# Norm operands made by VectorE, sums taken at other places, first squares in steps: a one-core transformer kernel

## The chip, the core and the metric

The kernel runs on one core of one Trainium2 chip. The metric is device microseconds of one execution. The core's engines work side by side, each through its own queue in order: TensorE (PE in the profile; PEld are its weight loads), VectorE (DVE), ScalarE (ACT), GpSimd (POOL) and SyncE (SP, which only starts transfers here).

## What is computed

The input is 256 tokens of 1024 numbers, in 32-bit floating point. Two blocks follow one another. The first is a norm, one wide projection, banded attention beside a gated recurrence, their merge and a feed-forward layer. The second has four more feed-forward layers, a gating unit and a second attention, each behind a norm of its own.

```python
def rmsnorm(x, g):
    var = jnp.mean(x * x, axis=-1, keepdims=True)
    return x * lax.rsqrt(var + 1e-6) * g

x = first_block(x, ...)                      # ends in a feed-forward layer (f0) and a final norm
for i in range(2):                           # second block
    if i == 1:
        k, v = split(rms_norm(x, kv_norm) @ w_kv)
    x = x + 0.5 * swiglu(rms_norm(x, ffn_norm[i, 0]), ...)       # f1, f3
    h = rms_norm(x, mix_norm[i])
    x = x + (chunked_sgu(h) if i == 0 else stick_breaking_attention(h @ w_q, k, v) @ w_o)
    x = x + 0.5 * swiglu(rms_norm(x, ffn_norm[i, 1]), ...)       # f2, f4
return rms_norm(x, final_norm)
```

Ahead of f1 stand two norms in a row: the first block's final norm and f1's own.

## The kernel before

The activations lie transposed, channels on the 128 partitions and the 256 tokens side by side: `X` is four tiles of 128 x 2 x 256. Weights come from memory as one stream of groups, 128 x 2048 numbers each (1 MB), in the order in which they are used (`PLAN`); a group is two chunks of 128 x 1024. TensorE multiplies in a rounded format, so every operand is held in two parts, a rounded high part and the rest as a low part. For a chunk of weights, ScalarE makes the high part (`h`, line 163) and VectorE subtracts it from the chunk (`l`, line 164); `prep` does both. A product is then three matmuls (`mm3`): high with high, high with low, low with high. A chunk is 24 such matmuls of 256 columns, nearly everywhere.

The order on every engine is the order in which the Python code issues the work. `group` issues the matmuls of two chunks; behind the first chunk it calls the hook `mid`, behind the second the hook `end`, and behind each it gives every waiting generator (`spawn`) two steps (`rounds`) and prepares up to `fills` chunks ahead (`refill`; 4 ahead at the start, 7 later). So a generator is a piece of work that is dealt out between the chunks.

A norm is not applied to its input. The layer behind it multiplies the unnormed input, and a factor R for each token is multiplied onto the result. R is found meanwhile:

1. `squares`: ScalarE squares the four tiles (line 274), VectorE adds them up (lines 276 and 277), and `hl_split` splits the sum into two parts in the tile rr: ScalarE copies the high part (line 337), VectorE subtracts (line 338).
2. `token_sums`: two matmuls with a matrix of minus ones (`nones`) sum over the partitions, into every row. VectorE takes the diagonal of the result (line 290) and reduces it (line 291) to one number for each token on a partition. GpSimd raises it to the power -1/2 (line 307, `rpow`).
3. `diag`: VectorE puts the factors on a diagonal (line 296), and `hl_split` makes two parts of it again.
4. `stats_b`: two more matmuls with `nones` spread the factors over all partitions, and ScalarE copies them to the tile R (line 328). Only then can the layer's results be multiplied (`mulR`, line 334).

`stats_a` is step 2 and asks for step 3 two rounds later; a feed-forward layer has four chunks in K order first (`start_k`), then calls `stats_a` behind the fifth chunk and `stats_b` behind the seventh. Three places matter here. In block 1 `squares` is issued as a whole ahead of the first matmuls. At f1 the two norms give two squares, and `early` takes both sums behind the fifth chunk. At the second attention, `stats_a` is issued behind the four chunks of the key and value projection (`kv`), and `diag` in slot 0 of the loop in `stick` that deals out the attention's work.

Of the kernel before, what the change touches and what calls it, by code (L numbers as in the profile page):

```python
# [9 lines left out]
F32 = mybir.dt.float32  # L10
F32R = mybir.dt.float32r
BF16 = mybir.dt.bfloat16
AF = mybir.ActivationFunctionType
ALU = mybir.AluOpType
# [92 lines left out]
class Builder:  # L107
# [163 lines left out]
    def squares(self, src, dst, n=0):  # L271
        nc = self.nc
        for p in range(4):
            nc.scalar.activation(dst[p], src[p], AF.Square)
        for p in range(1, 4):
            nc.vector.tensor_tensor(dst[0], dst[0], dst[p], op=ALU.add)  # L276
        nc.vector.tensor_tensor(dst[0][:, 0, :], dst[0][:, 0, :], dst[0][:, 1, :], op=ALU.add)
        self.hl_split(dst[0][:, 0, :], self.RR[0][:, n, :], self.RR[0][:, n + 1, :])

# [13 lines left out]
    def diag(self, col, s, n=0):  # L293

        d = s[1][:, 1, :]
        self.nc.vector.tensor_tensor(d.rearrange("p (a b) -> p a b", b=128), self.ident.unsqueeze(1).to_broadcast([128, 2, 128]),
                                     col.unsqueeze(2).to_broadcast([128, 2, 128]), op=ALU.mult)
        self.hl_split(d, self.RR[0][:, n + 2, :], self.RR[0][:, n + 3, :])

# [14 lines left out]
    def stats_a(self, pool=None, kv=False, wait=2):  # L314

        nc = self.nc
        self.st = (pool or self.acc)()
        self.R, self.rcol = (self.Rkv, self.rckv) if kv else (self.Rt, self.rc)
        self.token_sums(self.v2, self.st, self.sq)
        nc.vector.tensor_scalar(self.v2, self.v2, -1.0 / D, 1e-6, op0=ALU.mult, op1=ALU.add)  # L320
        self.rpow(self.rcol, self.v2)
        if wait is not None:
            self.spawn(self.later(wait, lambda: self.diag(self.rcol, self.sq)))

# [80 lines left out]

    def start_k(self, kinds, outs, fills=((2, 2), (2, 2))):
        for gi in range(2):
            self.group(kinds, lambda c, h, l, s: self.pe_k(h, l, s[2], self.XS, outs), fills=fills[gi])


    def block1(self):
        nc, dram = self.nc, self.dram
        SA, SL, RR = self.SA, self.SL, self.RR
        g = lambda k: ("norm_mix_g", k)
        for p in range(4):
            self.split_h(p, self.X, g, self.XS)
            self.split_l(p, self.X, g, self.XS)
            self.prep(2 if p == 0 else 1)
        self.squares(self.X, self.sq)

# [337 lines left out]
    def ffn(self, n, fin, fin_l, stats=None, nat=False, more=None):  # L758
        nc = self.nc
# [4 lines left out]
        def ev(j, bank):  # L764
# [7 lines left out]
            else:  # L772
# [6 lines left out]
        self.start_k((("K", f"{n}_in"),) * 2, [b[0][:, 0, :], b[0][:, 1, :], b[1][:, 0, :], b[1][:, 1, :]],  # L779
                     ((2, 2), (0, 0)) if more else ((2, 2), (2, 2)))  # L780
        sa, sbb = stats or (self.stats_a, self.stats_b)
# [69 lines left out]
    def block2(self):  # L851
# [23 lines left out]
        def early():  # L875
            self.st = self.acc()
            self.R, self.rcol = self.Rt, self.rc
            self.token_sums(self.v2, self.st, self.sq)
            nc.vector.tensor_scalar(self.v2, self.v2, -1.0 / D, 1e-6, op0=ALU.mult, op1=ALU.add)
            self.rpow(r1c, self.v2)  # L880
            self.token_sums(s2[:, 2:4], self.acc(), sq2, 4)
            nc.vector.tensor_tensor(s2[:, 2:4], s2[:, 2:4], r1c, op=ALU.mult)
            nc.vector.tensor_tensor(s2[:, 2:4], s2[:, 2:4], r1c, op=ALU.mult)
            nc.vector.tensor_scalar(s2[:, 2:4], s2[:, 2:4], -1.0 / D, 1e-6, op0=ALU.mult, op1=ALU.add)
            self.rpow(s2[:, 0:2], s2[:, 2:4])
            nc.vector.tensor_tensor(self.rc, s2[:, 0:2], r1c, op=ALU.mult)
            self.spawn(self.later(2, lambda: self.diag(self.rc, self.sq), lambda: self.diag(r1c, sq2, 4)))

# [16 lines left out]
        fin, fin_l = self.boundary(0.5, lambda k: ("mix_norm", k))  # L905
        self.ffn("f1", fin, fin_l, stats=(early, sbb), more=True)
        self.squares(self.X, self.sq)
# [28 lines left out]
        def kv_emit(c, h, l, s):  # L936
            kp = s[2]
            XH, XL = KX
            for kk in range(2):
# [5 lines left out]
                for t in range(2):  # L945
# [3 lines left out]
                    self.mm(vb[:, t, :], XL[:, k, ts], h[:, sl], False, k == 7)  # L949

        for gi in range(2):
            self.group((("K", "kv"),) * 2, kv_emit)

        def kv_ev(R=self.R, rcol=self.rcol):
            nc.vector.tensor_tensor(Kt, kb, R.unsqueeze(1).to_broadcast([128, 2, 256]), op=ALU.mult)
            for t in range(2):
                nc.scalar.activation(Vt[:, t, :], vb[:, t, :], AF.Copy, scale=rcol[:, t:t + 1])
            yield
# [157 lines left out]
    def stick(self, Kt, Vt, fin, fin_l):  # L1116
# [65 lines left out]

        self.stats_a(self.wk, wait=None)
        at = lambda f, T: f(T) if 0 <= T < 8 else None
# [47 lines left out]
        for slot in range(17):  # L1232
            at(values, slot - 5)
            next(work, None)
            if slot == 0:
                zero = SL["b"][:, 1536:1664]
                nc.gpsimd.memset(zero, 0.0)
                for i in range(2):
                    for t in (sh[i], sl[i]):
                        nc.vector.tensor_copy(t[:, :, 0:128], zero.unsqueeze(1).to_broadcast([128, 2, 128]))  # L1240
                self.diag(self.rcol, self.sq)
            if slot == 1:
                self.stats_b()
                nc.scalar.preload_act_table_set("natural_log_exp_and_others")
# [130 lines left out]
```

## Time and profile before

| | |
|---|---|
| median of 3 runs (their span) | 1414.47 us (1407.7 to 1415.67) |
| the profiled execution | 1416.44 us, its span 1414.7 us |
| TensorE busy | 1398.4 us, 99% of the span |
| VectorE, ScalarE, GpSimd busy | 969.2, 740.2, 25.6 us |
| chain that ended last | TensorE 94%, VectorE 3%, ScalarE 1% |
| mean transfer rate | 184 GB/s |

The profile is of one execution, and its times count from the start of the span. Busy time of TensorE is modelled from pipelined matmuls, so it can be near 100% and still hide differences in the spacing of matmuls. A wait is named by what ended it. The granted clock is given as a share of full speed (1.00 is 2.4 GHz, 0.50 is 1.2 GHz).

### The profile page before, as it was taken

How to read it: one execution, taken by the hardware profiler on the slowest of the kernel's cores; microseconds unless marked ns; L12 is line 12 of the kernel's file. 1: busy time of each engine (PE TensorE's matmuls, PEld its weight loads, DVE VectorE, ACT ScalarE, POOL GpSimd, SP SyncE). 2: the span in 40 equal slices, each digit the busy share in tenths (PEclk: the TensorE clock that was granted, in tenths of full speed). 3: DMA queues.
4: the chain of work that ended last, by engine and by line, in shares of the span. 5: the costliest groups of instructions: out<-in, count | busy, mean ns of one | idle time of the engine just before them, and what ended most of it. 6: DMA issues, size and time to landing. Idle time of an engine off the chain costs nothing.

```text
span 1414.7 us, 26947 instructions
## 1 busy us (share of the span) xinstructions
PE 1398.4 (99%) x11515; PEld 1356.9 (96%) x11515; DVE 969.2 (69%) x1361; ACT 740.2 (52%) x1112; POOL 25.6 (2%) x57
## 2 busy tenths in 40 slices
PE   8999999999999999999999999999999999999998
PEld 8998999999999999998999999999999998999997
DVE  6977687766667765668685766668656677666663
ACT  5686565554445544446444544446544467544442
POOL 1000000000000000000000000000000000000000
PEclk9999999999999999999999999999999999999999
DMA  8566554655553555556545565554555552445551
GB/s 295 185 201 206 174 195 137 222 185 203 183 205 127 201 199 189 179 194 223 177 151 179 179 224 194 181 204 166 201 217 196 180 179 90 143 171 202 186 188 51
DMA packets 37624, 260.31 MB, mean 184 GB/s; under 512 B 4224, under 2 KB 4608, under 8 KB 7040
## 3 DMA queue, kind: packets, MB, share of 16 engines
q1 hardware_dynamic: 36288, 253.77, 50.7%
q0 software_dynamic: 1072, 4.72, 1.0%
q8 instruction: 90, 1.47, 0.4%
q14 instruction: 30, 0.25, 0.1%
q10 hardware_dynamic: 144, 0.10, 0.0%
HBM read 257.53 MB, written 1.05 MB: 183 GB/s over the span
## 4 chain that ended last, share of the span: by engine, by line
PE 94%; DVE 3%; ACT 1%; issue 1%; DMA 1%; SPq 0%; POOL 0%; POOLq 0%; ACTq 0%; DVEq 0%
PE wk L211 60%; PE acc L211 34%; DVE l L164 1%; DMA raw<-w 1%; ACT h L163 1%; DVE sb L276 0%; DVE xl L267 0%; PE acc L550 0%; DVE x L342 0%; DVE sc L862 0%; DVE sd L276 0%; PE wk L550 0%; DVE x L344 0%; SPq L381 0%; ACT rr L337 0%
## 5 line engine op out<-in xcount | busy, mean ns | idle before, releaser
L164 DVE TENSOR_TENSOR l<-raw,h 128x1024 fp32r<-128x1024 f32 (+1 forms) x479 | 571.5, 1220 | 245.5 <-ACT h L163 245.2
L211 PE MATMUL wk<-xh,h 128*128 128x256 f32 x2272 | 634.1, 279 | 1.7 <-ACT h L163 1.7
L211 PE MATMUL wk<-xh,l 128*128 128x256 f32 x2272 | 631.6, 278 | 1.5 <-DVE l L164 1.5
L211 PE MATMUL wk<-xl,h 128*128 128x256 f32 x2272 | 631.4, 278 | 0.0
L163 ACT ACTIVATE h<-raw 128x1024 fp32r<-128x1024 f32 (+1 forms) x479 | 485.3, 1045 | 39.6 <-PE acc L211 25.8
L211 PEld LDWEIGHTS wk<-xh,h 128*128 128x128 f32 x2272 | 428.1, 188 | 4.8 <-ACT h L163 2.1
L211 PEld LDWEIGHTS wk<-xh,l 128*128 128x128 f32 x2272 | 428.3, 189 | 2.2 <-DVE l L164 2.2
L211 PEld LDWEIGHTS wk<-xl,h 128*128 128x128 f32 x2272 | 429.4, 189 | 0.6
L211 PE MATMUL acc<-rr,h 128*128 128x256 f32 x2016 | 351.2, 278 | 0.0
L211 PEld LDWEIGHTS acc<-rr,h 128*128 128x128 f32 x2016 | 305.1, 188 | 2.1 <-issue 1.9
L211 PE MATMUL acc<-rr,l 128*128 128x256 f32 x1008 | 279.7, 277 | 0.0
L211 PEld LDWEIGHTS acc<-rr,l 128*128 128x128 f32 x1008 | 189.3, 188 | 0.0
L768 ACT ACTIVATE sa<-sa 128x256 f32<-128x256 f32 x110 | 45.4, 418 | 251.2 <-DVE sa L334 250.7
L337 ACT ACTIVATE rr<-sa 128x256 fp32r<-128x256 f32 (+1 forms) x122 | 52.7, 438 | 185.7 <-DVE sa L773 129.1
L334 DVE TENSOR_TENSOR sa<-wk,rt 128x512 f32<-128x512 f32 x92 | 62.3, 686 | 47.7 <-PE wk L211 47.1
L338 DVE TENSOR_TENSOR rr<-sa,rr 128x256 fp32r<-128x256 f32 (+1 forms) x122 | 54.2, 451 | 53.4 <-ACT rr L337 53.4
L211 PE MATMUL acc<-h,rr 128*128 128x512 f32 (+1 forms) x208 | 63.1, 374 | 0.0
L211 PEld LDWEIGHTS acc<-h,rr 128*128 128x128 f32 x208 | 38.5, 188 | 6.6
L262 ACT ACTIVATE xh<-x,par 128x256 fp32r<-128x256 f32 x56 | 25.0, 501 | 31.4 <-DVE x L344 16.2
L211 PE MATMUL acc<-l,rr 128*128 128x512 f32 (+1 forms) x104 | 38.9, 374 | 0.0
L773 DVE TENSOR_TENSOR sa<-sa 128x256 f32<-128x256 f32 x88 | 37.1, 429 | 0.0
L211 PE MATMUL wk<-rr,h 128*128 128x256 f32 x192 | 33.0, 277 | 0.0
(253 smaller groups left out, 995.6 us busy)
## 6 DMA issues: line engine op xcount, KB each, us to landing
raw<-w SPq DMA_DIRECT2D x237, 1024.0 KB, 5.0
sd<-bias POOLq DMA_DIRECT2D x8, 384.0 KB, 3.3
raw<-w SPq DMA_DIRECT2D x3, 512.0 KB, 8.8
sh<-gates SPq DMA_DIRECT2D x1, 1024.0 KB, 8.3
out<-sf SPq DMA_DIRECT2D x4, 256.0 KB, 2.2
x<-x SPq DMA_DIRECT2D x3, 256.0 KB, 8.0
raw<-w SPq DMA_DIRECT2D x2, 256.0 KB, 4.4
sa<-ws POOLq DMA_DIRECT2D x1, 512.0 KB, 3.7
```

The lines of the kernel that those rows point to most:

```text
L163: nc.scalar.activation(h[:, s], raw[:, s], AF.Copy)
L164: nc.vector.tensor_tensor(l[:, s], raw[:, s], h[:, s].bitcast(F32), op=ALU.subtract)
L211: self.nc.tensor.matmul(out, lhsT, rhs, start=start, stop=stop, skip_group_check=True)
L262: self.nc.scalar.activation(xs[0][:, k, :], src[p][:, f, :], AF.Copy, scale=self.par(*g(k)))
L334: self.nc.vector.tensor_tensor(dst, bank, self.Rpair(), op=ALU.mult)
L337: self.nc.scalar.activation(zh, src, AF.Copy)
L338: self.nc.vector.tensor_tensor(zl, src, zh.bitcast(F32), op=ALU.subtract)
L768: nc.scalar.activation(t[:, 0, :], t[:, 0, :], AF.Silu)
L773: nc.vector.tensor_tensor(t[:, 1, :], t[:, 0, :], t[:, 1, :], op=ALU.mult)
```

## The change

Four things change. `two_parts` takes the place of `hl_split` in `squares` and `diag`: VectorE now casts the high part itself. In block 1 `squares_in_steps` is a generator that issues two squares a step, then one add a step, then the split. At f1, `early` keeps the first norm's sums, which move behind the fourth chunk (the new hook `end` of `start_k`); the second norm's sums stay behind the fifth chunk (`sa`), and both diagonals follow at once, the first norm's ahead of the factors' product. At the attention, `stats_a` moves behind the third of kv's four chunks and asks for `diag` two rounds later; `stats_b` stays in slot 1, and the clears of the padding move from slot 0 to slot 1.

```diff
@@ squares @@
-        self.hl_split(dst[0][:, 0, :], self.RR[0][:, n, :], self.RR[0][:, n + 1, :])
+        self.two_parts(dst[0][:, 0, :], n)
+
+    def two_parts(self, src, n):
+        h, l = self.RR[0][:, n, :], self.RR[0][:, n + 1, :]
+        self.nc.vector.tensor_copy(h, src)
+        self.nc.vector.tensor_tensor(l, src, h.bitcast(F32), op=ALU.subtract)
+
+    def squares_in_steps(self, src, dst, n=0):
+        nc = self.nc
+        for p in range(4):
+            nc.scalar.activation(dst[p], src[p], AF.Square)
+            if p % 2:
+                yield
+        for p in range(1, 4):
+            nc.vector.tensor_tensor(dst[0], dst[0], dst[p], op=ALU.add)
+            yield
+        nc.vector.tensor_tensor(dst[0][:, 0, :], dst[0][:, 0, :], dst[0][:, 1, :], op=ALU.add)
+        yield
+        self.two_parts(dst[0][:, 0, :], n)
@@ diag @@
-        self.hl_split(d, self.RR[0][:, n + 2, :], self.RR[0][:, n + 3, :])
+        self.two_parts(d, n + 2)
@@ block1 @@
-        self.squares(self.X, self.sq)
+        self.spawn(self.squares_in_steps(self.X, self.sq))
@@ ffn, start_k: the hook end is called behind the fourth chunk @@
-                     ((2, 2), (0, 0)) if more else ((2, 2), (2, 2)))
+                     ((2, 2), (0, 0)) if more else ((2, 2), (2, 2)), more)
@@ block2 @@
             self.rpow(r1c, self.v2)
+
+        def sa():
             self.token_sums(s2[:, 2:4], self.acc(), sq2, 4)
...
             self.rpow(s2[:, 0:2], s2[:, 2:4])
+            self.diag(r1c, sq2, 4)
             nc.vector.tensor_tensor(self.rc, s2[:, 0:2], r1c, op=ALU.mult)
-            self.spawn(self.later(2, lambda: self.diag(self.rc, self.sq), lambda: self.diag(r1c, sq2, 4)))
+            self.diag(self.rc, self.sq)
...
-        self.ffn("f1", fin, fin_l, stats=(early, sbb), more=True)
+        self.ffn("f1", fin, fin_l, stats=(sa, sbb), more=early)
...
+        R, rcol = self.R, self.rcol
         for gi in range(2):
-            self.group((("K", "kv"),) * 2, kv_emit)
+            self.group((("K", "kv"),) * 2, kv_emit, mid=(lambda: self.stats_a(self.wk)) if gi else None)
@@ stick @@
-        self.stats_a(self.wk, wait=None)
...
-            if slot == 0:
+            if slot == 1:
+                self.stats_b()
                 zero = SL["b"][:, 1536:1664]
...
-                self.diag(self.rcol, self.sq)
-            if slot == 1:
-                self.stats_b()
```

VectorE's order at the start of block 1, before (sb holds the squares, rr_79 the two parts of the sum; l is the low part of a weight chunk):

```order
L164 TENSOR_TENSOR l<-raw,h 128x1024
L276 TENSOR_TENSOR sb<-sb 128x512 x3
L277 TENSOR_TENSOR sb<-sb 128x256
L338 TENSOR_TENSOR rr_79<-sb,rr_79 128x256
L164 TENSOR_TENSOR l<-raw,h 128x1024 x4
L290 TENSOR_TENSOR sb<-acc,ident 128x256
```

And the same place now; the last row takes what the sums' matmuls made:

```order
L164 TENSOR_TENSOR l<-raw,h 128x1024 x2
L294 TENSOR_TENSOR sb<-sb 128x512 x2
L164 TENSOR_TENSOR l<-raw,h 128x1024
L294 TENSOR_TENSOR sb<-sb 128x512
L296 TENSOR_TENSOR sb<-sb 128x256
L164 TENSOR_TENSOR l<-raw,h 128x1024
L283 CAST rr_79<-sb 128x256
L284 TENSOR_TENSOR rr_79<-sb,rr_79 128x256
L164 TENSOR_TENSOR l<-raw,h 128x1024
L310 TENSOR_TENSOR sb<-acc,ident 128x256
```

Three of the l parts that stood behind the two parts of the sum now stand ahead of them, between the adds.

VectorE's order at f1's start, before (sb and sd hold the two norms' squares, v_97 and s_5221 their sums, r1c and rc the factors):

```order
L164 TENSOR_TENSOR l<-raw,h 128x1024 x2
L290 TENSOR_TENSOR sb<-acc,ident 128x256
L291 TENSOR_REDUCE v_97<-sb 128x2
L879 TENSOR_SCALAR v_97<-v_97 128x2
L290 TENSOR_TENSOR sd<-acc,ident 128x256
L291 TENSOR_REDUCE s_5221<-sd 128x2
L882 TENSOR_TENSOR s_5221<-s_5221,r1c 128x2
L883 TENSOR_TENSOR s_5221<-s_5221,r1c 128x2
L884 TENSOR_SCALAR s_5221<-s_5221 128x2
L886 TENSOR_TENSOR rc<-s_5221,r1c 128x2
L296 TENSOR_TENSOR sb<-ident,rc 128x256
L338 TENSOR_TENSOR rr_79<-sb,rr_79 128x256
```

And now, from the second norm's reduction on (the two l parts and the first norm's rows stand ahead of these as before):

```order
L310 TENSOR_TENSOR sd<-acc,ident 128x256
L311 TENSOR_REDUCE s_5221<-sd 128x2
L904 TENSOR_TENSOR s_5221<-s_5221,r1c 128x2
L905 TENSOR_TENSOR s_5221<-s_5221,r1c 128x2
L906 TENSOR_SCALAR s_5221<-s_5221 128x2
L316 TENSOR_TENSOR sd<-ident,r1c 128x256
L283 CAST rr_79<-sd 128x256
L284 TENSOR_TENSOR rr_79<-sd,rr_79 128x256
L909 TENSOR_TENSOR rc<-s_5221,r1c 128x2
L316 TENSOR_TENSOR sb<-ident,rc 128x256
L283 CAST rr_79<-sb 128x256
L284 TENSOR_TENSOR rr_79<-sb,rr_79 128x256
```

The diagonal of r1c, which stood behind rc's, moved with its two parts ahead of the product rc.

TensorE's order at the end of kv, as a difference (acc takes keys and values, rr_81 and rr_82 are kv's input, rr_79 the two parts of the squares' sum):

```order
 L211 MATMUL acc<-l,rr_81 128x256
 L211 MATMUL acc<-h,rr_82 128x256
+L211 MATMUL wk<-rr_79,nones 128x256 x2
 L211 MATMUL acc<-rr_81,h 128x256
 L211 MATMUL acc<-rr_82,h 128x256
```

The two matmuls of the sums, which stood behind kv's fourth chunk, now stand behind its third.

## Rows read from the trace of the kernel before

**Rows 1.** The page, part 1, busy time, share and instructions of each engine.

```profile
PE 1398.4 (99%) x11515; PEld 1356.9 (96%) x11515; DVE 969.2 (69%) x1361; ACT 740.2 (52%) x1112; POOL 25.6 (2%) x57
```

**Rows 2.** Waits of TensorE's queue: total us, times, longest us.

```profile
PE acc L211 <- ACT rr L337: 2.6, 3, 1.2
```

**Rows 3.** Timeline of TensorE, 20.6 to 26 us: start, length, instruction.

```profile
21.31 0.39 PE L211 MATMUL wk<-xh,h 128*128 128x256 f32 x1 [0.38 <-ACT h L163]
...
22.57 0.39 PE L211 MATMUL wk<-xh,l 128*128 128x256 f32 x1 [0.76 <-DVE l L164]
...
25.27 0.40 PE L211 MATMUL acc<-rr,nones 128*128 128x256 f32 x2
```

**Rows 4.** Timeline of ScalarE, 13 to 40 us.

```profile
15.84 2.17 ACT L274 ACTIVATE sb<-x 128x512 f32<-128x512 f32 x4
19.89 0.42 ACT L337 ACTIVATE rr<-sb 128x256 fp32r<-128x256 f32 x1 [1.88 <-DVE sb L277]
```

**Rows 5.** Timeline of VectorE, 13 to 40 us.

```profile
17.12 2.28 DVE L276 TENSOR_TENSOR sb<-sb 128x512 f32<-128x512 f32 x3
```

**Rows 6.** DMA issues between 6.7 and 7.0 us, median us to landing.

```profile
raw<-w SPq DMA_DIRECT2D x1, 1024.0 KB, 10.5
```

**Rows 7.** Groups of instructions of VectorE, shapes apart: count, busy us, mean ns.

```profile
L338 DVE TENSOR_TENSOR rr<-sb,rr 128x256 fp32r<-128x256 f32 x16 | 6.8, 426 | 8.9 <-ACT rr L337 8.9
...
L1240 DVE CAST rr<-sb 128x256 fp32r<-128x256 f32 x4 | 0.9, 287 | 1.0 <-POOL sb L1237 1.0
```

**Rows 8.** Timeline of TensorE at f1's start, 453.9 to 466 us.

```profile
454.15 0.39 PE L211 MATMUL acc<-rr,nones 128*128 128x256 f32 x2
455.48 0.84 PE L211 MATMUL acc<-rr,nones 128*128 128x256 f32 x2 [0.94 <-ACT rr L337]
...
465.34 0.41 PE L211 MATMUL wk<-xh,h 128*128 128x256 f32 x1
```

**Rows 9.** Timeline of VectorE at f1's start, 449 to 466 us.

```profile
450.21 0.42 DVE L277 TENSOR_TENSOR sb<-sb 128x256 f32<-128x256 f32 x1
...
458.69 0.42 DVE L290 TENSOR_TENSOR sb<-acc,ident 128x256 f32<-128x256 f32 x1
...
462.01 0.16 DVE L886 TENSOR_TENSOR rc<-s,r1c 128x2 f32<-128x2 f32 x1 [0.80 <-POOL s L307]
```

**Rows 10.** Timeline of TensorE at the attention's start, 1143 to 1160 us.

```profile
1146.58 0.40 PE L211 MATMUL wk<-rr,nones 128*128 128x256 f32 x2
...
1153.20 0.97 PE L211 MATMUL wk<-rr,nones 128*128 128x256 f32 x2 [2.13 <-ACT rr L337]
...
1159.67 0.70 PE L211 MATMUL wk<-sd,sc 64*128 64x256 f32 x4
```

**Rows 11.** Timeline of VectorE at the attention's start, 1124 to 1172 us.

```profile
1142.90 0.43 DVE L277 TENSOR_TENSOR sb<-sb 128x256 f32<-128x256 f32 x1
...
1144.76 4.63 DVE L164 TENSOR_TENSOR l<-raw,h 128x1024 fp32r<-128x1024 f32 x4 [0.52 <-ACT h L163]
1149.31 0.42 DVE L290 TENSOR_TENSOR sb<-wk,ident 128x256 f32<-128x256 f32 x1
```

**Rows 12.** Windows: us, busy us (instructions) of engines, granted clock, DMA.

```profile
461.70:464.20 2.50, 1.05 (x5) 0.45 (x3) 1.35 (x4) 0.59 (x2) 0.28 (x1) 1.00 0.00 0
464.30:467.60 3.30, 3.10 (x13) 2.93 (x14) 2.60 (x4) 1.97 (x5) 0.00 (x0) 0.50 0.00 0
1153.80:1157.10 3.30, 3.30 (x16) 3.30 (x17) 2.08 (x3) 3.16 (x6) 0.00 (x0) 0.50 0.27 42
20.60:24.00 3.40, 2.26 (x17) 1.86 (x17) 2.88 (x4) 3.40 (x4) 0.00 (x0) 1.00 0.93 369
```

**Rows 13.** Chain in order of time: start us, us, what.

```profile
288.39 5.44 PE acc L211 x48
...
475.04 5.65 PE acc L211 x48
...
616.37 5.65 PE wk L211 x48
```

More of the change, by code (lines that the diff above doesn't have):

```diff
@@ L321, in stats_a @@
         self.rpow(self.rcol, self.v2)
-        if wait is not None:
-            self.spawn(self.later(wait, lambda: self.diag(self.rcol, self.sq)))
+        self.spawn(self.later(wait, lambda: self.diag(self.rcol, self.sq)))
     def stats_b(self):
@@ L404, in view, with start_k @@
         return [t[:, i * w:(i + 1) * w].rearrange("p (a b) -> p a b", b=256) for i in range(n)]
-    def start_k(self, kinds, outs, fills=((2, 2), (2, 2))):
+    def start_k(self, kinds, outs, fills=((2, 2), (2, 2)), end=None):
         for gi in range(2):
-            self.group(kinds, lambda c, h, l, s: self.pe_k(h, l, s[2], self.XS, outs), fills=fills[gi])
+            self.group(kinds, lambda c, h, l, s: self.pe_k(h, l, s[2], self.XS, outs), fills=fills[gi],
+                       end=end if gi else None)
     def block1(self):
@@ L949, in kv_emit, with kv_ev @@
                     self.mm(vb[:, t, :], XL[:, k, ts], h[:, sl], False, k == 7)
+        R, rcol = self.R, self.rcol
         for gi in range(2):
-            self.group((("K", "kv"),) * 2, kv_emit)
-        def kv_ev(R=self.R, rcol=self.rcol):
+            self.group((("K", "kv"),) * 2, kv_emit, mid=(lambda: self.stats_a(self.wk)) if gi else None)
+        def kv_ev():
             nc.vector.tensor_tensor(Kt, kb, R.unsqueeze(1).to_broadcast([128, 2, 256]), op=ALU.mult)
```

## The prediction

> **What bounds the kernel now.** I read the page's share of busy time first: TensorE is busy 1398.4 of 1414.7 us [rows 1]. So a change can win only where TensorE stands still or runs slower than it could, and three views show these places. The list of TensorE's waits is short; its longest row is 2.6 us in three waits for ScalarE's copies into rr, the operands of the norms' sums [rows 2], which the rows of TensorE's order of time place at f1's start [rows 8]; one more such wait of 2.13 us stands at the attention's start [rows 10], and at block 1's start it waits 0.38 us for an h and 0.76 us for an l [rows 3]. The second view is the granted clock: right behind f1's waits and behind the attention's it is 0.50 for a whole stretch, while around block 1's it stays at 1.00 [rows 12]. The third is the chain in order of time: 48 matmuls of 256 columns take 5.44 us in f0 and 5.65 us all the way through f1, both at full clock [rows 13]. The slower spacing (117.7 ns for 113.3 ns) is there from the first such row behind f1's waits to the last one at 616 to 622 us, so a wait can cost more after it than in itself.
>
> **The sum's base** is the profiled execution, 1416.44 us = span 1414.7 + 1.74 around it. The two timed runs near it (1414.47, 1415.67) lie 1 to 2 us lower; the third, 1407.7, is 8.7 lower.
>
> **Two parts by VectorE, everywhere.** Before, ScalarE copies the high part; the copy takes 0.42 us [rows 4], but it waits in ScalarE's queue for VectorE's adds, and every h behind it waits too. After, VectorE casts and subtracts: a cast of this shape takes 287 ns, a subtract 426 ns [rows 7]. Nine squares and nine diagonals (16 of the 18 subtracts are in that row) make 18 casts, 5.2 us more on VectorE in the whole run; it is 69% busy [rows 1], and its l parts are the cover: where I use them below they are ready before TensorE asks. Without that cover, each cast would cost its 0.29 us. Outside the three places TensorE waits for no sums, so there I cost the edit at nothing.
>
> **Block 1's start.** Before, the four squares end at 15.84 + 2.17 = 18.0 us, the copy starts only at 19.89, and the next h (for the fifth chunk) at about 20.3 [rows 4]; TensorE waits for it and its l [rows 3] and takes the sums at 25.27. After, that h comes right behind the squares, 18.0 to 19.05 (its transfer took 10.5 us from about 6.9, so it is there at 17.4 [rows 6]). VectorE makes the l by 20.25, before TensorE asks near 21.0: those two waits go. But the sums' operands come later. VectorE's order now has in front of them an l, two adds, an l, two adds, an l. An l takes 4.63 / 4 = 1.16 us [rows 11], an add 2.28 / 3 = 0.76 [rows 5], the halving add 0.42 [rows 9]: from 20.25 the adds end at 21.7, the l at 22.85, the adds at 23.95, the l at 25.1; cast 25.35, subtract 25.8. TensorE ended the chunk before at 21.31 - 0.38 = 20.93 [rows 3]; matmuls overlap a little, so without the wait the fifth chunk starts near 20.8, and its 24 matmuls are through at 20.8 + 24 x 0.1133 = 23.5. It waits 1.85 us for the high part and another 0.35 for the low, and goes on near 26.0, where before it went on two matmuls behind 25.27, at 25.5 [rows 3]. **Term: +0.5 us**; bounds -0.3 (operands 0.8 sooner) to +2.1 (this wait halves the clock as at f1, where 3.30 us were at 0.50 [rows 12] and so about 1.6 lost). Behind the sums stand the next l and the diagonal, which had 2 us of waits for ScalarE and lose them.
>
> **f1's start.** Before, the first norm's sums run at 454.15, the second's wait for the copy until 455.48, the factors' matmuls wait for two more copies, and the layer's matmuls go on at 465.34, at half clock [rows 8]. After, the first pair stands one chunk earlier, at 454.15 - 24 x 0.1133 = 451.43. Its adds end at 450.63 [rows 9], cast 450.95, subtract 451.4: in time. The second block's adds follow without a copy between: 451.35 to 453.6 and 454.1, cast 454.4, subtract 454.85. TensorE asks for them at 454.4 to 454.5 and waits about 0.4, in place of 0.94 and more. Then two l parts (2.3 us) to 457.1, where the first row of the sums' chain starts; before, that was 458.69 [rows 9], so the chain starts 1.6 us sooner. From there to rc it took 462.01 - 458.69 = 3.3 us, so rc could come at 460.4; the other diagonal with its parts now stands ahead of it, fills the time of the power on GpSimd and holds rc to 460.6; then rc's diagonal, cast and subtract end at 461.25, 461.55 and 462.0. TensorE reaches them at 460.6, waits 1.0 and 0.35, and goes on at 462.5 instead of 465.34: 2.85 us. The clock: before, 1.05 busy of 2.50 us came ahead of the fall [rows 12]; now the idle time is about 1.4 us, as at block 1's start before (2.26 busy of 3.40, no fall), so I take no fall: from 465.34 to 467.6 the 2.3 us at half clock become about 1.2, another 1.05. **Term: -3.9 us**; bounds -2.4 (the clock falls) and -4.7 (no wait for the second pair, and a chain 0.4 shorter).
>
> A rule speaks against this place. The power on GpSimd and the first diagonal now run at once, which no row of before has. The Trainium skill (SBUF — State Buffer, section Who interferes with whom) says that VectorE's two-input operations from SBUF and its two-port casts share a port with GpSimd, and that the later one stands still until the earlier is done. By it the cast would wait out the power and the low part come at 462.7 instead of 462.0, the sum 0.7 us higher. No run here shows it.
>
> **The attention's start.** Before, the sums run behind the kv chunks at 1146.58, but VectorE's reduction waits behind four l parts until 1149.31, and the factors come at 1153.2 after 2.13 us of waiting, with the clock at 0.50 behind it [rows 10 to 12]. After, the sums stand one chunk earlier (near 1143.8). Adds end at 1143.3 [rows 11], cast 1143.65, subtract 1144.1: a new wait of 0.3 us there. Two l parts now stand ahead of the reduction instead of four, and the four clears of the padding go behind the diagonal: reduction 1146.4 to 1147.4, power to 1148.2, an l, diagonal and parts done at 1149.7. TensorE asks at 1151.2: no wait. From 1146.6, where kv ended before, to the first scores (1159.67 before [rows 10]) stand the new wait of 0.3 us, the two matmuls of the sums, two of the factors and 72 of q: 0.3 + 76 x 0.1133 = 8.9 us, so the scores start at 1155.5. **Term: -4.1 us**; bounds -3.0 (half of the wait comes back at the clears or the kv evictions, now behind two l parts) and -4.4 (no new wait).
>
> **Sum:** +0.5 - 3.9 - 4.1 = -7.5, or 1408.9 against the profiled 1416.44; for a timed run of the same kind, about a microsecond lower, **1408**.
>
> **Rivals.** (A) The forecast: the waits shrink, but f1's start still has some, and f1 runs at the slower spacing behind them as before. (B) The same sum, but f1 at the faster spacing: from 463 to 633 us, 170 x (1 - 5.44/5.65) = 6.3 us more [rows 13], **1402**. For it: the spacing is a state that a layer keeps and not a property of its work, since f0 has the same matmuls at the faster one; what sets it at a wait no row shows, so a shorter wait may end in either; and the timed run at 1407.7 is about 7 under its fellows, which this would explain. Against it: it was slow behind both waits of f1 in this trace, and three of four executions of before lie at the high level. (C) The change doesn't make the sums sooner where it counts: f1's chain keeps VectorE's two l parts in front, and the clock falls there and at block 1: +2.1 - 2.4 - 4.1 = -4.4, by the same base **1411**. For it: the same l parts do stand there. (D) The other side: one new wait, the 0.3 us for the sums inside kv or a like one at f2's or f3's start, leaves TensorE at the slower spacing through two layers of f1's length that now run at the faster: 340 x (5.65/5.44 - 1) = +13, so 1408 + 13 = **1421**. It decides once VectorE's parts come later than TensorE's sums there. Against it: outside the three places the chain got shorter by a hand-over, and the sums had no waits.
>
> **Chances.** A 0.44, B 0.42, C 0.10, D 0.04. Half a per cent, 7.1 us of 1414.47 (about what a measurement here can tell from no change), is at 1407.4. B is faster; of A (1406 to 1411, by the terms' bounds) about a quarter lies under that. So faster 0.53, within 0.43, slower 0.04. The range runs from 1400 (B with block 1 at the faster spacing as well, 1 us) to 1412.5 (C and its bound); D and the tails, about 0.15, are left out.
>
> **What would show it.** In the changed profile: no wait for h or l at 21 to 22.6 us but one for the sums near 23.5; VectorE's first reduction in f1 1.6 us earlier against the end of f0; TensorE waits of about 1.4 us in f1 and a clock of 1.00 there; no wait for the factors in attention, scores about 4 us sooner; 48 matmuls in f1 at 5.65 (A) or 5.44 us (B). I am wrong if the clock falls at block 1's new wait, if f1's chain is held by GpSimd, or if the spacing changes in a layer where no wait was.

## The result and the profile after

The changed kernel takes 1402.47 us in the median (14 runs, 1400.62 to 1408.83), the kernel before 1409.84 us (14 runs beside them, 1407.7 to 1415.67). The ratio is 0.9944, with a 95% interval of 0.9926 to 0.9962: faster by 0.56%; the medians differ by 7.4 us. The profiled execution took 1405.7 us, its span 1404.0.

Part 1 of the page, as in [rows 1], and the list of what TensorE's queue waited for, as in [rows 2]:

```profile
PE 1390.9 (99%) x11515; PEld 1350.0 (96%) x11515; DVE 972.4 (69%) x1379; ACT 734.3 (52%) x1094; POOL 26.5 (2%) x57
```

```profile
PE acc L211 <- DVE rr L283: 2.4, 2, 1.6
PE wk L211 <- ACT h L163: 1.3, 1, 1.3
PE wk L211 <- DVE sc L413: 1.1, 1, 1.1
PE wk L211 <- DVE l L164: 1.0, 2, 0.8
PE wk L211 <- ACT sh L1188: 0.5, 1, 0.5
```

The waits for ScalarE's copies into rr are gone (2.6 and 2.1 us). Two waits for VectorE's cast (line 283) remain, one in block 1 and one at f1's start. They stand in TensorE's timeline (start, length, instruction, idle time ahead of it), first block 1, then f1, then the attention:

```profile
22.14 0.28 PE L211 MATMUL wk<-xh,l 128*128 128x256 f32 x1
23.97 0.85 PE L211 MATMUL acc<-rr,nones 128*128 128x256 f32 x2 [1.55 <-DVE rr L283]
24.65 0.28 PE L211 MATMUL wk<-xh,h 128*128 128x256 f32 x1
...
449.92 0.42 PE L211 MATMUL acc<-rr,nones 128*128 128x256 f32 x2
453.03 0.76 PE L211 MATMUL acc<-rr,nones 128*128 128x256 f32 x2
460.07 1.07 PE L211 MATMUL acc<-rr,nones 128*128 128x256 f32 x4 [0.84 <-DVE rr L283]
460.98 0.28 PE L211 MATMUL wk<-xh,h 128*128 128x256 f32 x1
...
1132.01 0.76 PE L211 MATMUL wk<-rr,nones 128*128 128x256 f32 x2
1139.50 0.39 PE L211 MATMUL wk<-rr,nones 128*128 128x256 f32 x2
1143.90 0.93 PE L211 MATMUL wk<-sd,sc 64*128 64x256 f32 x8
```

Where two matmuls of 256 columns take 0.42 or 0.39 us, their operands were there; 0.76 us says that the second pair of f1's sums (453.03) and the attention's sums (1132.01) waited some 0.35 us for their low part. VectorE's timeline shows the chain behind these times: in block 1 the adds between the l parts (line 294 adds in steps, 296 halves), and in f1 the reductions (310), the first diagonal with its parts (316, 283, 284), then rc's.

```profile
18.97 1.41 DVE L294 TENSOR_TENSOR sb<-sb 128x512 f32<-128x512 f32 x2
20.30 1.22 DVE L164 TENSOR_TENSOR l<-raw,h 128x1024 fp32r<-128x1024 f32 x1
21.44 0.68 DVE L294 TENSOR_TENSOR sb<-sb 128x512 f32<-128x512 f32 x1
22.15 0.42 DVE L296 TENSOR_TENSOR sb<-sb 128x256 f32<-128x256 f32 x1
22.50 1.22 DVE L164 TENSOR_TENSOR l<-raw,h 128x1024 fp32r<-128x1024 f32 x1
23.63 0.28 DVE L283 CAST rr<-sb 128x256 fp32r<-128x256 f32 x1
...
455.53 0.42 DVE L310 TENSOR_TENSOR sb<-acc,ident 128x256 f32<-128x256 f32 x1
...
457.96 0.42 DVE L316 TENSOR_TENSOR sd<-ident,r1c 128x256 f32<-128x256 f32 x1
458.41 0.29 DVE L283 CAST rr<-sd 128x256 fp32r<-128x256 f32 x1
...
459.73 0.29 DVE L283 CAST rr<-sb 128x256 fp32r<-128x256 f32 x1
```

GpSimd's second power in f1, which runs beside that first diagonal, and its power in block 1 with the l part that VectorE was at:

```profile
458.13 0.79 POOL L327 TENSOR_TENSOR s<-s,mhalf 128x2 f32<-128x2 f32 x1 [0.76 <-DVE s L906]
...
26.42 1.22 DVE L164 TENSOR_TENSOR l<-raw,h 128x1024 fp32r<-128x1024 f32 x1
...
26.59 1.62 POOL L327 TENSOR_TENSOR rc<-v,mhalf 128x2 f32<-128x2 f32 x1 [23.52 <-DVE v L340]
```

The granted clock (third number from the right) stays at 1.00 behind all three places, where [rows 12] had 0.50 behind f1's and the attention's waits:

```profile
22.20:24.60 2.40, 0.77 (x4) 0.38 (x4) 2.37 (x5) 1.74 (x2) 0.00 (x0) 1.00 1.01 355
...
461.00:464.30 3.30, 3.30 (x32) 3.30 (x31) 3.30 (x7) 2.30 (x7) 0.00 (x0) 1.00 0.45 127
...
1144.00:1147.30 3.30, 3.30 (x30) 3.12 (x31) 1.81 (x2) 2.52 (x5) 0.00 (x0) 1.00 0.57 169
```

The chain in order of time gives the spacing, as in [rows 13]: 48 matmuls take 5.45 us in block 1 behind its sums, 5.44 us all through f1, and 5.65 us in f4, the last layer.

```profile
24.82 5.45 PE wk L211 x48
...
469.31 5.44 PE acc L211 x48
...
605.30 5.44 PE wk L211 x48
...
1222.62 5.65 PE wk L211 x48
1380.63 5.66 PE wk L211 x48
```

**A ledger of all kernels.** TensorE has 11,515 matmul records in every trace. The table takes the starts of the 113th, 346th, 3874th, 5258th, 9644th and last of them, and gives the us between (in the kernel before these starts are at 18.05, 47.06, 470.05, 633.05, 1160.21 and 1407.65 us). No pair of sums crosses such a border. The experiments follow below.

| kernel | block 1 | to f1's start | f1 | to the attention's scores | rest, with f4 | profiled run |
|---|---|---|---|---|---|---|
| before | 29.01 | 422.99 | 163.00 | 527.15 | 247.44 | 1416.44 |
| changed | 28.59 | 419.09 | 156.85 | 523.09 | 252.47 | 1405.7 |
| changed, second | 30.27 | 419.11 | 156.85 | 523.11 | 247.46 | 1402.83 |
| changed, third | 28.60 | 419.10 | 156.85 | 523.07 | 247.44 | 1401.09 |
| parts by VectorE alone | 27.09 | 421.39 | 156.85 | 524.53 | 247.44 | 1403.69 |
| attention as before | 30.18 | 419.25 | 163.00 | 524.63 | 247.44 | 1410.38 |
| f1's start as before | 28.28 | 419.77 | 156.85 | 523.11 | 247.45 | 1401.65 |
| copies by ScalarE | 31.63 | 422.57 | 163.00 | 523.64 | 247.49 | 1414.75 |
| first squares whole | 27.21 | 419.24 | 163.00 | 523.10 | 252.47 | 1411.25 |
| parts behind the l | 26.70 | 419.10 | 156.85 | 523.09 | 247.45 | 1399.72 |
| the same, second | 26.64 | 419.11 | 156.85 | 523.07 | 247.45 | 1399.44 |
| f1's preparations behind | 26.98 | 417.84 | 156.85 | 523.09 | 247.45 | 1399.96 |
| both | 26.68 | 417.85 | 156.85 | 523.07 | 247.44 | 1398.38 |
| both, second | 26.41 | 417.99 | 163.00 | 523.47 | 247.38 | 1404.38 |

Between before and the changed kernel's first profile: 1.23 us ahead of block 1's column (its start lies between 16.82 and 18.95 us in the fourteen profiles; why was not followed), 0.42 in block 1, 3.90 at f1's start, 6.15 in f1, 4.06 at the attention, and 5.03 given back in f4. There is one profile of the kernel before, so how often its clock falls behind f1's and the attention's waits is not shown.

### The profile page after: what moved, and what is told of

It is laid out like the page before. It is cut to its first block, busy times and chain, and to the rows that moved or that the text cites. A ratio compares the mean times of both kernels' runs of the same rounds, so it can differ in the third digit from the quotient of the medians.

```text
span 1404.0 us, 26948 instructions
## 1 busy us (share of the span) xinstructions
PE 1390.9 (99%) x11515; PEld 1350.0 (96%) x11515; DVE 972.4 (69%) x1379; ACT 734.3 (52%) x1094; POOL 26.5 (2%) x57
## 4 chain that ended last, share of the span: by engine, by line
PE 95%; DVE 3%; ACT 1%; issue 1%; DMA 1%; SPq 0%; POOLq 0%; POOL 0%; DVEq 0%; ACTq 0%
PE wk L211 60%; PE acc L211 35%; DVE l L164 1%; DMA raw<-w 1%; ACT h L163 0%; DVE sb L276 0%; PE acc L570 0%; DVE x L361 0%; DVE rr L284 0%; DVE sc L882 0%; ACT sb L290 0%; DVE sd L276 0%; PE wk L570 0%; SPq L400 0%; DVE sb L294 0%
```

## The experiments

All ratios are to the kernel before, from runs on the same chip. The kernels are named as in the table.

**1. Parts by VectorE alone.** Every sum stands where it stood; the first squares are whole.

```diff
 diag, and squares likewise:
-        self.hl_split(d, self.RR[0][:, n + 2, :], self.RR[0][:, n + 3, :])
+        self.two_parts(d, n + 2)
```

> The kernel before with one part of the change: VectorE casts and subtracts both parts of every norm operand; the sums in the second feed-forward layer and in attention stand where they stood, and the first squares are handed out whole. Theory (the gain comes from TensorE's two stalls being taken away by the earlier sums): only the hand-over to ScalarE's copy goes, so TensorE still waits for the second pair of sums and the factors in f1 (together 1.5 to 2.5 us instead of 3.5) and 1.7 to 2.1 us for the factors in attention, with the clock at 0.50 behind the latter; the time is 1 to 2.5 us under before. Rival (the gain comes from ScalarE being relieved everywhere): most of the 7 us is here, 5 to 7 us under before.

Measured: median 1408.25 us (12 runs, lowest 1402.38), ratio 0.9971 (0.9954 to 0.9989). The timeline of TensorE, f1's factors and then the attention's, and the clock in the windows behind them:

```profile
459.06 0.85 PE L211 MATMUL acc<-rr,nones 128*128 128x256 f32 x2 [0.63 <-DVE rr L283]
460.28 0.75 PE L211 MATMUL acc<-rr,nones 128*128 128x256 f32 x2 [0.37 <-DVE rr L283]
...
1141.99 0.84 PE L211 MATMUL wk<-rr,nones 128*128 128x256 f32 x2 [1.21 <-DVE rr L283]
```

```profile
461.30:464.60 3.30, 3.30 (x18) 3.30 (x17) 3.23 (x7) 2.03 (x7) 0.00 (x0) 0.50 0.50 149
1142.00:1145.30 3.30, 3.22 (x26) 3.03 (x27) 2.83 (x4) 2.40 (x4) 0.00 (x0) 1.00 0.26 45
```

The theory's waits are there for f1 (1.0 us in all, where 1.5 to 2.5 was said), but the attention's wait is 1.21 instead of 2.13 us and the clock does not fall behind it. By the table block 1 wins 1.92 us, f1's start 1.60 and the attention 2.62: 6.1 us, more than the theory's 1 to 2.5. Some 1.5 us of the attention's share is the clock that stays up: behind the old wait 16 matmuls took 3.30 us [rows 12], 1.8 us at 113.3 ns each. The timed runs decide less: the ratio is worth 1.6 to 6.5 us, the medians differ by 1.2. In the profiles the rival's size holds; its reason (relief everywhere) does not, since the last column is as long as before, and f1's differs by the spacing alone.

**2. Attention as before** and **3. f1's start as before**, each in the changed kernel.

```diff
 2:
-            self.group(..., kv_emit, mid=(lambda: self.stats_a(self.wk)) if gi else None)
+            self.group(..., kv_emit)
...
+        self.stats_a(self.wk, wait=None)
 3:
-            self.diag(r1c, sq2, 4)
...
-            self.diag(self.rc, self.sq)
+            self.spawn(self.later(2, lambda: self.diag(self.rc, self.sq), lambda: self.diag(r1c, sq2, 4)))
...
-        self.ffn("f1", fin, fin_l, stats=(sa, sbb), more=early)
+        self.ffn("f1", fin, fin_l, stats=(early, sbb), more=True)
```

> The changed kernel, but attention's sums, its diagonal and its clears stand where they stood before. Theory: the factors' wait at the scores is back with 1.7 to 2.1 us and the clock falls to 0.50 behind it, so the stretch from kv's end to the first scores is 3 to 4 us longer than in the changed kernel, and the time 3 to 4 us above it (3 to 4.5 us under before). Rival (ScalarE relieved everywhere): within 1 us of the changed kernel. Second rival (the spacing of the matmuls carries the gain and is set by the stalls): more than 6 us above it.

> The changed kernel, but the sums and diagonals of the second feed-forward layer stand where they stood before. Theory: the waits for the second pair and for the factors are back (about 2 us more idle, and 1 us more if the clock falls to 0.50), and the time is 2.5 to 4 us above the changed kernel at the same spacing of the matmuls. Rival (relief of ScalarE): within 1 us. Second rival (the stall at f1's start sets the slower spacing for the whole layer): 48 matmuls in f1 take 5.65 us again in every execution and the time is 9 to 10 us above the changed kernel.

Measured: attention as before 1408.58 us (12 runs, lowest 1402.38; ratio 0.9977, 0.9954 to 1.0000); f1's start as before 1404.37 us (12 runs, lowest 1401.2; ratio 0.9965, 0.9947 to 0.9983). The stretches are longer than the changed kernel's by 1.54 us at the attention and by 0.67 us at f1's start, both under what the theory said. The attention's wait of 1.21 us is back, with no fall of the clock. At f1 the waits are those of experiment 1 (0.63 and 0.37 us), but here the window behind them is at full clock:

```profile
461.30:464.60 3.30, 3.23 (x26) 3.06 (x27) 3.30 (x6) 1.33 (x4) 0.00 (x0) 1.00 0.16 37
```

So the same waits took the clock down in the profile of experiment 1 (421.39 us to f1's start) and not in this one (419.77): a difference of 1.6 us that the waits don't account for. The medians, 6.4 and 2.2 us above the changed kernel's on that chip (1402.21, experiment 9), are mixed of the groups of runs that experiment 9 is about, so they don't measure these stretches. The second rival, that the stall sets f1's spacing, falls: f1 is at 156.85 us in experiment 3, where its sums stand late again, and at 163.00 in experiment 2, which has f1's start as the change has it. Nor is it the fall of the clock: f1 is at 156.85 us behind the fall in experiment 1, and at 163.00 without one in experiment 2.

**4. Copies by ScalarE**, the reverse of experiment 1: sums and steps as in the change.

```diff
 two_parts:
-        self.nc.vector.tensor_copy(h, src)
-        self.nc.vector.tensor_tensor(l, src, h.bitcast(F32), op=ALU.subtract)
+        self.hl_split(src, self.RR[0][:, n, :], self.RR[0][:, n + 1, :])
```

> The changed kernel with the hand-over left in: ScalarE copies the high part of every norm operand as before, while the sums stand sooner and the first squares in steps as in the change. From the runs so far: at f1's start the stretch from the end of the first chunks to the matmuls behind the factors took 17.03 us before, 13.67 with VectorE's parts alone and 12.95 with both; from kv's end to the scores 15.15, 12.61 and 10.79 us. Theory (each sum waits for the later of two things, and the hand-over is the larger share): f1 15 to 16.5 us, attention 11.5 to 13.5 us, the time 2 to 4 us under before. Rival (the sooner sums alone do it, the hand-over only matters where they stand late): within 1 us of the changed kernel. Second rival (ScalarE's queue holds the sooner copies longer than the later ones): f1 or attention no shorter than before.

Measured: 1406.57 us (12 runs, lowest 1402.95), ratio 0.9981 (0.9959 to 1.0003). At f1's start TensorE still waits for ScalarE's copies, of the second sums and of the factors, and the clock is at 0.50 behind them (467.2 to 470.4 us):

```profile
457.70 0.85 PE L211 MATMUL acc<-rr,nones 128*128 128x256 f32 x2 [0.68 <-ACT rr L354]
465.75 1.08 PE L211 MATMUL acc<-rr,nones 128*128 128x256 f32 x4 [1.55 <-ACT rr L354]
```

Against the kernel before, f1's start wins 0.42 us, the attention 3.51, and block 1 loses 2.62, with a wait of 1.19 us for the copy, one of 0.64 for the low part, and the clock at 0.50 from 26.8 to 30.2 us. In the narrower cut that its expectation uses (3777th to 3874th and 9551st to 9644th record, which a pair of sums worth 0.2 us leaves by standing sooner) f1 takes 16.41 us, in the theory's range, and the attention 11.17, under it; the first rival falls, as the third run of the changed kernel on the same chip has 1401.05 us. Together with experiment 1: at f1's start VectorE's parts alone (no hand-over) give 1.6 us (3.2 without the fall of the clock, by experiment 3), the sooner sums alone 0.4, both 3.9; at the attention 2.6, 3.5 and 4.1, so there either of them does most of it, since either keeps the clock up, which is some 1.5 us of each.

**5. First squares whole** and **6. parts behind the l**, both in the changed kernel.

```diff
 5:
-        self.spawn(self.squares_in_steps(self.X, self.sq))
+        self.squares(self.X, self.sq)
 6:
-        self.spawn(self.squares_in_steps(self.X, self.sq))
+        for p in range(4):
+            nc.scalar.activation(self.sq[p], self.X[p], AF.Square)
+        for p in range(1, 4):
+            nc.vector.tensor_tensor(self.sq[0], self.sq[0], self.sq[p], op=ALU.add)
+        nc.vector.tensor_tensor(self.sq[0][:, 0, :], self.sq[0][:, 0, :], self.sq[0][:, 1, :], op=ALU.add)
+        self.spawn(self.later(2, lambda: self.two_parts(self.sq[0][:, 0, :], 0)))
```

> The changed kernel, but block 1's squares and their adds are handed out whole, ahead of the next h and l. Theory: VectorE's adds come ahead of the fifth chunk's l, so TensorE waits 0.5 to 1 us for that l at 21 to 22 us, and no longer 1.5 + 0.46 us for the sums' operands: the layer gets on 1 to 1.5 us sooner than in the changed kernel. Rival (the steps are a gain, because the wait for the l is longer than that for the sums): TensorE waits 2 us or more there, and the time is 0.5 us or more above the changed kernel.

> The changed kernel, but in block 1 the squares and adds are handed out whole and only the cast and the subtract of the sums' operand stand behind the next l. Theory: with the adds ahead of the fifth chunk's l and its two parts behind it, TensorE waits neither for that l (at most 0.2 us, where it waited 0.7 us with everything whole) nor for the sums, so block 1 gets on about 2.2 us sooner than in the changed kernel: its lowest runs near 1398.5. Rival (the weights' transfers bound this stretch, and a wait taken away here comes back as one for the next h or l): no gain over the kernel with whole squares, lowest runs at 1400.

Measured: whole squares 1403.64 us (12 runs, lowest 1400.06; ratio 0.9959, 0.9939 to 0.9980); parts behind the l 1402.46 us (6 runs, lowest 1399.72; ratio 0.9932, 0.9908 to 0.9956). With whole squares TensorE waits for the fifth chunk's l and then for nothing:

```profile
20.88 0.39 PE L211 MATMUL wk<-xh,l 128*128 128x256 f32 x1 [0.53 <-DVE l L164]
23.49 0.39 PE L211 MATMUL acc<-rr,nones 128*128 128x256 f32 x2
```

Block 1 takes 27.21 us there and 26.70 with the parts behind the l, for 28.6 in the changed kernel (30.27 in its second profile): 1.4 and 1.9 us. The steps cost what the theory said, and the last half microsecond is that wait for the l. The time follows less than was expected of it: the lowest runs are 0.5 and 0.8 us under the changed kernel's 1400.56. In part that is what lies ahead of block 1's column (17.24 and 17.60 us in these profiles, 16.82 to 17.26 in the changed kernel's); the rest is open.

**7. f1's preparations behind** the two diagonals, and **8. both** of 6 and 7.

```diff
-                     ((2, 2), (0, 0)) if more else ((2, 2), (2, 2)), more)
+                     ((0, 0), (0, 0)) if more else ((2, 2), (2, 2)), more)
...
-                           ..., fills=(0, 1) if more and i < 4 else (2, 2),
+                           ..., fills=(2 if i == 2 else 0, 1) if more and i < 4 else (2, 2),
```

> The changed kernel, but the two l preparations that stand ahead of the norm's chain in the second feed-forward layer are handed out behind its two diagonals. Theory (the two l parts hold the chain up): the wait for the factors' matmuls in f1 (1.0 us and 0.35 us for the low part) goes, no wait for an l takes its place, and the time is 1.3 us under the changed kernel at the same spacing. Rival (the l parts are needed at once): TensorE waits 1 us or more for an l in f1 in place of the factors, and the time is the same or longer.

> Both of the last two edits in one kernel. Theory: the gains add up, 2.2 + 1.3 = 3.5 us under the changed kernel, lowest runs near 1397 and the ratio to before about 0.992. Rival (each only moves a wait to a later place): within 1 us of the changed kernel.

Measured: f1's preparations behind 1407.51 us (12 runs, lowest 1399.82; ratio 0.9968, 0.9944 to 0.9991); both 1404.72 us (7 runs, lowest 1398.38; ratio 0.9944, 0.9924 to 0.9964). In the profiles the theory holds: the four factors' matmuls of f1 take 0.62 us with no wait (they are the row below), no l is waited for in their place, and f1's start is 1.25 us shorter than in the changed kernel. With both, block 1 and f1's start are 3.2 us shorter together, of 3.5 expected, and the lowest run is 2.2 us under the changed kernel's.

```profile
459.60 0.62 PE L211 MATMUL acc<-rr,nones 128*128 128x256 f32 x4
```

Yet the medians are above the changed kernel's: most timed runs of both kernels lie 6 us or more over their lowest.

**9. The changed kernel twice more**, **both**, and **parts behind the l** once more each, unchanged.

> The changed kernel itself, once more. Theory (the spacing of the matmuls is set anew in each execution, separately for f1 and for f4, whatever the waits): its runs fall again into groups some 5 to 6 us apart, lowest near 1400.9, and the profile need not show f4 at the slower spacing (48 matmuls in 5.65 us) as the first one did. Rival (the change makes f4 slow and f1 fast): f4 is slow and f1 fast again, and all runs of the first profile's kind lie at one level.

> The kernel with both edits (block 1's two parts behind the next l, f1's preparations behind the diagonals) once more, beside the changed kernel on the same chip. Theory: at the same spacing of the matmuls it is 2.2 us under the changed kernel (lowest runs near 1398.4), while its median moves with the share of runs in which f1 or f4 is at the slower spacing (6.2 and 5.0 us). Rival (the moved preparations make the slower spacing in f1 more frequent): most runs lie near 1404.6 again and the median is no lower than the changed kernel's.

> The changed kernel a third time, as the partner of the last run. Theory: lowest runs near 1400.6, groups 5 to 6 us above; whether f1 or f4 is at the slower spacing in its profile is open (of ten profiles so far f1 was slow in three and f4 in two). Rival: the state belongs to the kernel, and f1 is at the faster spacing as in its two profiles before.

> The kernel in which only block 1's two parts are moved behind the next l, once more, to see whether it beats the changed kernel (28 timed runs: median near 1401.4, 20 of them under 1403.5). Theory: block 1's waits are gone in every execution (no fall of the clock there), lowest runs near 1399.7, and with f1's start left as in the change most runs lie under 1402, so its median is 0.5 to 1.5 us under the changed kernel's. Rival (an earlier arrival at f1 changes how often f1 comes out at the slower spacing, as it did when f1's preparations were moved): half of the runs or more lie near 1405, and the median is above the changed kernel's.

Measured: changed, second 1402.21 us (6 runs; ratio 0.9934, 0.9909 to 0.9959); third 1401.05 us (8 runs; 0.9939, 0.9916 to 0.9963); both, second 1404.63 us (11 runs; 0.9950, 0.9931 to 0.9970); parts behind the l, second 1399.55 us (6 runs, 1399.32 to 1400.07; 0.9929, 0.9911 to 0.9948). The chain of the changed kernel's second profile shows f4 at the faster spacing, where the first had the slower:

```profile
1223.89 5.44 PE wk L211 x48
1377.99 5.47 PE wk L211 x48
```

The chain of both, second, shows f1 at the slower one, from right behind the second pair of sums on and with no wait for the factors:

```profile
421.05 5.44 PE wk L211 x48
451.95 5.65 PE wk L211 x48
466.55 5.65 PE acc L211 x48
...
607.88 5.65 PE wk L211 x48
```

So one kernel comes out at either spacing in f4, and one in f1; the changed kernel's own f1 was at the faster one in all three profiles, as the third run's rival had it. By their times, runs with neither layer slow lie under 1403.5 us in these kernels: 20 of the changed kernel's 28 and 9 of the 12 with the parts behind the l, but only 6 of the 30 in which f1's preparations were moved (experiments 7 to 9; beside one another 7 of 8 of the changed kernel and 2 of 11 of both). The spacing is drawn anew in each execution, then, and the counts speak for the rival, that what stands at f1's start changes the odds. They don't show it: of these longer runs only one was profiled, and the attention as before, whose f1 starts as the changed kernel's does, has 4 of 12 under 1405 us, the like border with its 1.5 us more.

**The better version** is probably parts behind the l. Of the runs with neither layer slow its 9 lie at 1399.32 to 1400.35 us, the changed kernel's 20 at 1400.56 to 1403.48, and block 1 is 1.9 us shorter. That its median is lower too (1399.90 us for 1401.43) is not shown to be its doing: the runs come from different chips, and beside one another the two had 1402.46 and 1402.21. At equal spacing both would be the fastest (lowest 1398.38), but it seldom is at equal spacing.

## Why the prediction was right

The time of 1402.47 us lies in the range, and the terms were said to save 7.5 us and the medians differ by 7.4. The forecast itself, 1408, was 5.5 us too high, by its base and not by its terms; B's 1402 meets the time.

**Block 1, +0.5 us.** The waits for h and l at 21 to 22.6 us went, and one for the sums came: 1.55 us and then about 0.45 for the low part (the pair starts 0.68 us ahead of the next matmul, where two that wait for nothing make 0.23), where the prediction had 1.85 and 0.35, from 23.5 on. The column says -0.42, but in the kernel before these matmuls ran at the slower spacing (48 in 5.65 us at 25.67, against 5.45 at 24.82 in the changed one), which is worth about 0.8 us over the 22 us behind the sums, so +0.4 at like spacing. Whether that spacing is chance is open: of the fourteen profiles the two with ScalarE's copies (before and experiment 4) have 5.65 us there and the twelve others 5.44 or 5.45, so the 0.8 us may be a gain of VectorE's parts that no term had. The upper bound, a fall of the clock, is real too: in the second profile the window behind the same wait is at 0.50, and the stretch takes 30.27 us. First the row of before, then that profile's windows:

```profile
25.67 5.65 PE wk L211 x48
...
22.20:25.50 3.30, 1.63 (x12) 1.23 (x12) 3.23 (x6) 2.00 (x2) 0.00 (x0) 1.00 1.00 370
25.70:29.00 3.30, 3.30 (x17) 3.30 (x17) 2.63 (x6) 0.00 (x0) 1.62 (x1) 0.50 0.70 223
```

What the term hid is that it is a sum of a gain and a loss: VectorE's parts alone make block 1 1.9 us shorter (experiment 1; 1.1 at like spacing), and the steps take 1.5 of it back (28.60 against 27.09).

**f1's start, -3.9 us.** Measured 3.90, and by its steps: no wait for the first pair, 0.35 for the second (0.4 said), 0.84 and about 0.45 for the factors (1.0 and 0.35 said; the four start 0.91 us ahead of the next matmul, where unhindered ones make 0.45), a clock of 1.00. In the trace of before the power's result rc was reached 3.3 us behind the chain's first row; after, 3.55 (455.53 to 459.08), as worked out.

**The attention, -4.1 us.** Measured 4.06: some 0.35 us of wait for the sums' low part (0.3 said), no wait for the factors, full clock. This term and f1's each hold a fall of the clock in the one profile of before (some 1.5 and 1.1 us). None of the seven profiles with f1's start as in the change shows a fall there.

**Two parts elsewhere, nothing.** The rest with f4 takes 247.44 us before and in the profiles with f4 at the faster spacing, and VectorE is at 69% as it was. What the prediction did not see, because it priced each place as a whole, is which edit pays: at f1 and in block 1 it is VectorE making both parts, and not the other edits (experiments 1 and 4).

**The base, and A against B.** This is the step that missed. The sum was set against the profiled 1416.44 us and lowered by a microsecond, on the ground that three of four executions of before lay at the high level. Of 100 runs of before, made beside all these kernels, 58 are at 1410.2 us or under and the median is 1409.6: 1409.6 - 7.5 is 1402.1. The table agrees: the three places give 8.4 us, 7.6 without block 1's spacing. So A's wait was right and A's spacing was not: f1 was at the faster one in all three profiles of the changed kernel, as in B. But B's 6.3 us aren't shown to be a gain of the change: f1 was at the slower spacing in five of the fourteen profiles of the table, with and without waits for the factors, and by its timed runs the kernel before comes near 1408 us too. That the time is B's is thus no proof of B's reason.

**C and D.** C did not come: the chain of f1 came 1.6 us sooner against f0's matmuls, and the clock held at f1. D's price appeared (5.03 us in f4, in a layer with no new wait), but in one of three profiles of the same kernel, so it does not come with the change each time. Two of the prediction's three signs of being wrong thus came, each in one profile of the three: this one, and the fall of the clock at block 1's wait (1.7 us, inside that term's bound).

**The rule on the shared port.** The prediction set the Trainium skill (SBUF — State Buffer, Who interferes with whom) against its sum, for 0.7 us. In f1 the cast at 458.41 lies wholly inside GpSimd's power (458.13 to 458.92) and took its 0.29 us; rc's low part ended 4.95 us behind the chain's first row, where the row sum had 4.9. By this trace the rule did not hold VectorE there. The other way round the trace agrees with the rule: in the changed kernel's first profile a power takes 0.55 to 0.72 us, but each of the seven that start while VectorE runs a two-input operation from SBUF ends 0.54 to 0.58 us behind that operation. In block 1 the l part ends at 27.64 and the power at 28.21, in f1 the first diagonal's product (457.96 and 0.42 us) at 458.38 and the power at 458.92. So it was GpSimd, the later of the two, that was held, by about 1 us in block 1 and 0.1 in f1. The prediction says rightly that before has no power beside the first diagonal, but before has one beside an l part too (27.00, 1.62 us), from which this could be read.

**Right in its sum, open in its cause.** What sets a layer's spacing to 113.3 or 117.8 ns (156.85 or 163.00 us for f1's 1384 matmuls) is not settled; neither the waits nor a fall of the clock at its start do it alone. Nor was it tried why the same waits lower the clock in one execution and not in the next.

## What to carry to other kernels

A small copy on another engine's queue is paid for by its place in that queue: moving the high part to the engine that makes the low part shortened three stretches by 1.6 to 2.6 us, with what the spacing and the clock added there. Asking sooner gave 0.4 us at f1 and 3.5 at the attention, where the wait had been longest. Work that is dealt out in steps between the l parts reaches a consumer later than work handed out whole; look at which of the two the consumer asks for first. And before a profiled time is taken as the base of a sum, see whether the timed runs lie in groups, and in which group the profile is.

## What the runs showed of the hardware

The same three-part matmuls of 256 columns run at 113.3 or 117.8 ns at full clock for a whole layer: f1 takes 156.85 or 163.00 us and the rest with f4 247.45 or 252.47, and nothing in between was seen in the profiles. One kernel shows either of them. The timed runs lie in groups 5 to 6 us apart, as these differences would make them, where the whole change gains 7.4. The share of runs in each group differs between kernels, so that both, whose first profile is 1.3 us shorter than that of parts behind the l (1398.38 for 1399.72), had the higher median.

The same waits (0.63 and 0.37 us) were followed by a granted clock of 0.50 in one profile and of 1.00 in another, a difference of 1.6 us in that stretch.

A GpSimd power of 128x2 that started while VectorE made an l part took 1.50 to 1.62 us, and 0.55 to 0.72 us where no two-input operation was running; VectorE's operations beside it kept their length (1.22 us for the l, 0.29 for the cast).
